# A float32 decoder layer on one core: low parts of split operands emitted a step after their conversions

## The chip, the core and the metric

The kernel runs on one core of a Trainium2 chip. The metric is device time in microseconds, the median of three runs. Engines are named as in the profile: PE (TensorE matmul), PEld (its weight loads), DVE (VectorE), ACT (ScalarE), POOL (GpSimd), SP (SyncE, here only a queue that issues DMAs).

## What is computed

One layer of a decoder over 512 tokens of 2048 features: a gated mix of sparse attention and latent attention, cross attention over 256 memory tokens, and an MLP of 8192 features. Cut to its frame:

```python
xn = rmsnorm(h, g_mix[l])
(q_a, k_c, v_c, k_s, v_s, k_w, v_w, g_nsa, c_q, c_kv, k_r,
 gate_a, gate_b) = jnp.split(xn @ w_in[l], bounds, axis=-1)
...
o_a = nsa_attention(q_a, kc, vc, ks, vs, kw, vw, gates, ...)   # 16 heads: compressed, selected, window branch
o_b = mla_attention(c_q, c_kv, k_rope, ...)                    # 16 heads from latents of 512 and 256
mixed = sigmoid(gate_a) * (o_a @ w_o_nsa[l]) + sigmoid(gate_b) * (o_b @ w_o_mla[l])
h = h + mixed @ w_out[l]
h = h + memory_cross_attention(rmsnorm(h, g_xattn[l]), rmsnorm(mem, g_mem[l]), ...)
hn = rmsnorm(h, g_mlp[l])
h = h + jnp.square(jax.nn.relu(hn @ w_ff1[l])) @ w_ff2[l]
return rmsnorm(h, g_final)
```

## The kernel before

**Split operands.** Every large product is float32 made of three products of a rounded type (fp32r): an operand x is kept as a high part, hi = round(x), and a low part, lo = round(x - hi), and `mm` (L460 to L462) adds hi·hi, hi·lo and lo·hi. `split` (L467 to L471) makes the two: a conversion on ACT writes hi, a subtraction on DVE reads x and hi and writes lo. The subtraction is emitted right after the conversion, so DVE, which works in order, stands at it until ACT has come to the conversion.

**Order.** The program is one list of instructions written out by hand; each engine takes its own in that order and waits by semaphores for the others'. A main stream of projections runs through `chunk` and `ft`; after each group of three products they call `Side.run`, which takes steps of side work at a set rate: attention steps, and "post" steps that turn a finished projection into heads.

**Weights.** `Stream` loads units of 512 KB into a ring of two raw areas (`RAW`) and splits them, half a unit per call, into a ring of three split areas (`HLB`), about two units ahead of their use: `get` splits one half, `mid`, called in the middle of a unit, the other. `done` says that a raw area is free, once both halves of its unit have been split; the load of the unit two later is issued from there, on SP's queue (in the output projection also on POOL's, adding in place). A unit is 24 full products of 512 columns in most stages.

**Heads.** `proj_post` (sparse attention), `heads_T` (latent attention) and `proj_m`'s `post` (latents) transpose 128 x 128 blocks with PE into one PSUM bank of the pool `st`, and `split` that bank. `st` has three banks in rotation; `new_st` takes the next, and the first product into it waits until its last reader is done. `proj_m` also squares the latents' rows on ACT (L1135, L1137), the four row blocks in one step.

**Attention.** `scores` makes a branch's score rows from the last block to the first, one bank each; `soft` takes a row's maximum on DVE (L609) and the exponential on ACT (L610); one step later the row is scaled on DVE (L628). In the compressed branch the compressed scores share a bank with the row's, but for the last block (512 columns, a full bank), where they take one more. `values` transposes the softmax weights in groups (`tr`, L705) into a bank, splits them, and multiplies them with the values two steps later (`pv`, L724, L726). `attend` merges the score steps of a branch with the value steps of the one before.

**The end.** The MLP is a Strassen-like scheme of products p; `prep` loads and splits weights three steps ahead (L1635, L1640), `use2` adds or subtracts a product's sums from the result rows on DVE (L1867, L1869). Around the last two products the result is normalized: `square` (ACT, L1969), `rstd`, then one half of a row block is scaled by `factor` (DVE, the gain) and `scaled` (ACT, the row's factor), the other half by `both` (DVE, L1991), each followed by the store. Rows 0 and 1 finish beside the last product but one, rows 2 and 3 in `end`.

Of the kernel before, what the change touches and what calls it, by code (L numbers as in the profile page):

```python
# [16 lines left out]
EPS = 1e-6  # L17
# [236 lines left out]
class Stream:  # L254
# [4 lines left out]
    def __init__(self, k, dram_w, order, info):  # L259
        self.k, self.dram, self.order, self.info = k, dram_w, order, info  # L260
        self.raw = [k.slots.get() for _ in range(self.RAW)]
        self.hl = [(k.slots.get(), k.slots.get()) for _ in range(self.HLB)]
        self.n = self.nd = self.ns = self.nr = self.warm = 0
# [27 lines left out]
    def done(self, t):  # L291
        return self.ns >= 2 * self.user.get(id(t), -1) + 2
# [17 lines left out]
    def _split(self, upto):  # L310
# [3 lines left out]
        while self.ns < upto and self.ns < 2 * self.last:  # L314
# [6 lines left out]
            self.k.split(HL(h[:, s], l[:, s]), self.at[n][:, s])  # L321
            self.ns += 1
            if half:
                t = self.at.pop(n)
# [14 lines left out]
    def end(self):  # L339
        for t in [*self.raw, *(t for h in self.hl for t in h)]:  # L340
            self.k.slots.put(t)

    def get(self, tag):
# [6 lines left out]
        self._split(2 * (n + self.HLB) - 1)  # L350
        c = self.info[dram(tag)][1]
# [16 lines left out]
class Side:  # L368


    def __init__(self):
# [26 lines left out]
    def run(self, n, post):  # L398
        if post and self.post is not None:
# [10 lines left out]
    def drain(self):  # L410
        self.end_post()
        while self.step():
            pass
        self.acc = 0


class Layer:
    def __init__(self, tc, ctx, a, order, info):
# [36 lines left out]
        self.side = Side()  # L455
# [19 lines left out]

    def new_st(self):
        return self.psst.tile([128, 512], F32, name="st")
# [74 lines left out]
    def heads_T(self, n, take):  # L552

        for v in range(n):
# [8 lines left out]
            self.split(h, ps[:96, :])  # L563
            take(h)
            yield

# [48 lines left out]
    def scores(self, item):  # L615
# [27 lines left out]
        def step(i):  # L643
# [5 lines left out]
            elif i >= 0 and not (i == 0 and "stats" in item):  # L649
                o, n = at(i)  # L650
                ps = self.new_st()
                pc = None
# [4 lines left out]
                elif i < 3:  # L657
                    self.mm(ps[:, :32 + n], qi, k[:, :32 + n], True, True)
                    pc, ps = ps[:, :32], ps[:, 32:32 + n]
# [6 lines left out]
                if cgate:  # L666
                    self.soft(pc, item["Pc"][:, i], self.cst[:, C_CM + i * 32:C_CM + i * 32 + 32], SC_ATT,
                              cmx[:, i:i + 1], csm[:, i:i + 1])
# [16 lines left out]
    def values(self, item):  # L685
# [6 lines left out]
        def tr(group):  # L692
# [17 lines left out]
            else:  # L710
                self.split(h[:, :o], ps[:, :o])
# [26 lines left out]
    def attend(self, items, start=None):  # L738
# [3 lines left out]
        for it in items:  # L742
# [4 lines left out]
            for f in merge(a, b, LEAD):  # L747
                f()
                yield
# [5 lines left out]
    def flush(self):  # L755
        for f in self.values(self.prev):
            f()
# [124 lines left out]
    def proj_post(self, c):  # L882
# [34 lines left out]
        for nm, x in (("q", None), ("ks", 1), ("kw", 2)):  # L917
            for i, o in at.get(nm, ()):
# [11 lines left out]
                self.split(h, ps[:96, :])  # L930
                yield
        if c == 1:
# [186 lines left out]
    def proj_m(self, rate):  # L1119
# [10 lines left out]
        def post(c):  # L1130
# [9 lines left out]
            yield  # L1140
            for j in range(3):
# [9 lines left out]
                self.split(h, ps, self.gains[:, G_Q + f:G_Q + f + 1])  # L1151
                (self.cq if f < 4 else self.ckv).append(h)
                yield
            if c:
# [416 lines left out]
class Mlp:  # L1571
# [164 lines left out]
    def run(self, out):  # L1736
# [11 lines left out]
        for p in range(last):  # L1748
# [14 lines left out]
            for j in range(4):  # L1763
# [33 lines left out]
        self.end(last, X)  # L1797
# [128 lines left out]
    def end(self, p, X):  # L1926

        k, nc = self.k, self.nc
        v = nc.vector
        for t in (2, 3):  # L1930
            self.square(t, 2)
            self.square(t, 3)
            self.factor(t, 1)
# [4 lines left out]
        self.square(2, 1)  # L1938
        for j in range(4):
# [3 lines left out]
        self.scaled(2, 1, r2)  # L1943
        self.both(2, 0, r2)
# [38 lines left out]
    def scaled(self, t, b, r):  # L1983
# [3 lines left out]
        nc.scalar.dma_start(self.out[t][:, 1024 * b:1024 * b + 1024], x)  # L1987
# [68 lines left out]
```

## Time and profile before

| | |
|---|---|
| median of 3 runs | 2831.62 us (2830.07 to 2833.07) |
| profiled execution | 2828.84 us, its span 2827.0 us, TensorE clock 0.999 |
| DMA | 460.19 MB, mean 163 GB/s |
| PE, chain that ended last | 93% of the span |

A row of the stage table gives the stage, its length, each engine's busy time with its count of instructions, the granted clock, the DMA share and the rate. Rows of waits give the sum in us, how often, and the longest. Rows of groups give busy time, mean ns of one, and the idle time of the engine before them with what ended it. Rows in order of time give start, duration, and in brackets the idle time of the engine just before. In names, `st`, `mm` and `o` are PSUM banks, `s` and `d` areas of SBUF, `PP` the softmax rows, `mx` the row maxima.

### The profile page before, as it was taken

To read this page: it belongs to the slowest core of one execution; us is meant where nothing else is said; L and a number is where in the kernel's file an instruction comes from. 1 tells how busy PE (TensorE), PEld (TensorE's weight loads), DVE (VectorE), ACT (ScalarE), POOL (GpSimd) and SP (SyncE) were. 2 spreads that over 40 slices of the span, in tenths; PEclk is the share of its full clock that TensorE was granted. 3 is DMA by queue.
4 is the path that set the end of the run, shared out by engine and by line. 5 is a ranking of instruction groups with operands and counts; after the bars stand their busy time and mean duration, and the time that the engine had idled before them with its cause. 6 is when DMAs were issued, how large, how long until landed. Compare 5 with 4: busy or idle time off the path is not lost.

```text
span 2827.0 us, 38143 instructions
## 1 busy us (share of the span) xinstructions
PE 2799.2 (99%) x14091; PEld 2378.8 (84%) x14091; DVE 1915.9 (68%) x3160; ACT 1514.7 (54%) x2611; POOL 412.8 (15%) x626
## 2 busy tenths in 40 slices
PE   9999999999999999999999999999999999999998
PEld 8888889888888888889998888888888888888886
DVE  6446666665555565556785877777766788888787
ACT  5445555544444444334566766666666644444445
POOL 4130011002010001001130111111111111111110
PEclk9999999999999999999999999999999999999999
DMA  5331112222333335559644888798888999889996
GB/s 179 96 96 61 59 54 64 60 94 91 96 101 101 97 121 192 183 182 255 161 105 142 216 221 209 204 223 212 213 211 205 229 229 226 227 225 236 239 236 164
DMA packets 151883, 460.19 MB, mean 163 GB/s; under 512 B 16144, under 2 KB 32912, under 8 KB 151696
## 3 DMA queue, kind: packets, MB, share of 16 engines
q1 hardware_dynamic: 82736, 271.05, 28.6%
q0 software_dynamic: 41472, 151.01, 28.4%
q10 hardware_dynamic: 27488, 35.70, 3.6%
q8 instruction: 110, 1.80, 0.3%
q14 instruction: 77, 0.63, 0.1%
HBM read 419.94 MB, written 37.75 MB: 162 GB/s over the span
## 4 chain that ended last, share of the span: by engine, by line
PE 93%; DVE 3%; ACT 3%; issue 1%; DMA 0%; SPq 0%; ACTq 0%; DVEq 0%
PE mm L460 12%; PE mm L462 12%; PE mm L461 12%; PE mm L1821 8%; PE mm L1823 8%; PE mm L1822 8%; PE st L1823 5%; PE st L1821 5%; PE st L1822 5%; PE st L705 2%; DVE s L468 1%; PE o L724 1%; PE mm L1422 1%; PE mm L1421 1%; PE mm L1420 1%; PE o L726 1%
## 5 line engine op out<-in xcount | busy, mean ns | idle before, releaser
L460 PE MATMUL mm<-s,s 128*128 128x512 f32 (+5 forms) x1528 | 601.2, 393 | 1.1 <-ACT s L1127 0.7
L461 PE MATMUL mm<-s,s 128*128 128x512 f32 (+5 forms) x1528 | 582.5, 381 | 0.6 <-DVE s L468 0.4
L462 PE MATMUL mm<-s,s 128*128 128x512 f32 (+5 forms) x1528 | 582.7, 381 | 0.0
L468 DVE TENSOR_TENSOR s<-s,s 128x512 fp32r<-128x512 f32 (+4 forms) x558 | 384.2, 711 | 225.5 <-ACT s L467 224.5
L467 ACT CAST s<-s 128x512 fp32r<-128x512 f32 (+4 forms) x558 | 330.0, 608 | 257.9 <-PE mm L461 84.2
L1821 PE MATMUL mm<-s,s 128*128 128x512 f32 x1024 | 400.1, 391 | 3.0 <-DVE s L1869 3.0
L1823 PE MATMUL mm<-s,s 128*128 128x512 f32 x1024 | 398.5, 389 | 0.0
L1822 PE MATMUL mm<-s,s 128*128 128x512 f32 x1024 | 398.5, 389 | 0.0
L1640 DVE TENSOR_TENSOR s<-s,s 128x1024 fp32r<-128x1024 f32 x234 | 284.1, 1222 | 151.7 <-ACT s L1635 151.2
L462 PEld LDWEIGHTS mm<-s,s 128*128 128x128 f32 x1528 | 287.2, 188 | 53.4 <-DVE s L471 0.4
L461 PEld LDWEIGHTS mm<-s,s 128*128 128x128 f32 x1528 | 288.6, 189 | 40.5 <-DVE s L468 2.1
L460 PEld LDWEIGHTS mm<-s,s 128*128 128x128 f32 x1528 | 287.8, 188 | 40.8 <-ACT s L870 1.3
L1635 ACT CAST s<-s 128x1024 fp32r<-128x1024 f32 x234 | 241.9, 1048 | 128.5 <-DMA s<-wts 111.5
L610 ACT ACTIVATE PP<-PP,mx 128x512 f32<-128x512 f32 (+2 forms) x208 | 116.3, 559 | 285.2 <-DVE mx L609 285.2
L1821 PE MATMUL st<-s,s 128*128 128x512 f32 x672 | 263.1, 391 | 0.0
L1823 PE MATMUL st<-s,s 128*128 128x512 f32 x672 | 261.7, 389 | 0.0
L1822 PE MATMUL st<-s,s 128*128 128x512 f32 x672 | 261.4, 389 | 0.0
L1821 PEld LDWEIGHTS mm<-s,s 128*128 128x128 f32 x1024 | 192.3, 188 | 42.6 <-issue 3.4
L1635 ACT CAST s<-d 128x1024 fp32r<-128x1024 f32 x138 | 143.2, 1048 | 155.9 <-DMA d<-wts 141.6
L1823 PEld LDWEIGHTS mm<-s,s 128*128 128x128 f32 x1024 | 192.3, 188 | 40.0
L1822 PEld LDWEIGHTS mm<-s,s 128*128 128x128 f32 x1024 | 192.3, 188 | 39.2
L468 DVE TENSOR_TENSOR s<-st,s 128x384 fp32r<-128x384 f32 (+2 forms) x201 | 123.7, 621 | 123.8 <-ACT s L467 123.1
(342 smaller groups left out, 4813.9 us busy)
## 6 DMA issues: line engine op xcount, KB each, us to landing
s<-wts SPq DMA_DIRECT2D x312, 512.0 KB, 3.8
s<-wts POOLq DMA_DIRECT2D x149, 512.0 KB, 8.3
d<-wts POOLq DMA_DIRECT2D x91, 512.0 KB, 8.6
PP<-wts POOLq DMA_DIRECT2D x48, 512.0 KB, 8.6
d<-wts SPq DMA_DIRECT2D x47, 512.0 KB, 7.8
d_u<-s ACTq DMA_DIRECT2D x64, 256.0 KB, 5.2
PP<-wts SPq DMA_DIRECT2D x28, 512.0 KB, 8.1
d<-d_u SPq DMA_DIRECT2D x19, 512.0 KB, 8.8
```

Source lines behind the costliest of these rows:

```text
L460: t.matmul(ps, a.hr, b.hr, start=first, stop=False)
L461: t.matmul(ps, a.hr, b.lr, start=False, stop=False)
L462: t.matmul(ps, a.lr, b.hr, start=False, stop=last)
L467: nc.scalar.copy(o.hr, src)
L468: nc.vector.tensor_sub(o.lr, src, o.hi)
L610: nc.scalar.activation(p, p, AF.Exp, bias=mx, scale=-1.0, accum_out=sm)
L705: nc.tensor.transpose(ps[:rows, o:o + 128], p, self.ident)
L1635: self.nc.scalar.copy(t.hr, self.raw[i])
L1640: self.nc.vector.tensor_sub(t.lr, r, t.hi)
L1821: m(ps, a.hr, b.hr, start=first, stop=False, skip_group_check=True)
L1822: m(ps, a.hr, b.lr, start=False, stop=False, skip_group_check=True)
L1823: m(ps, a.lr, b.hr, start=False, stop=last, skip_group_check=True)
```

## The change

- `Stream._split` emits the conversion alone and remembers the half; the new `_low` emits the subtraction of the half before (all of them for a unit that `get` hands out). `done` now counts subtractions (`nl`), and the load of a later unit and the release of an area move into `_low`.
- `split_late` does the same for heads, latents and softmax weights: it emits the conversion and puts the subtraction on a list with the count of `st` banks taken so far and a number of groups, `runs`. `tick`, called by every `Side.run`, emits those whose groups have passed (2 for heads and latents); `attend` and `flush` emit before each attention step all whose number is used up (softmax weights, 0); `new_st` emits whatever still reads the bank that it is about to give out; `settle` at the end of a post step emits the rest.
- In the compressed branch the last block's compressed scores go into columns 416 to 448 of the third block's bank, one step later, and take no bank of their own.
- `proj_m`'s squares: one row block per step, four steps for one.
- At the end: the last weights' low part (`prep`), the first two rows' `both` and the gain products (`factor`) move behind the subtractions of the product before (`use2`) and behind the third row's additions; the third row's `both` moves behind the last addition; its other half is stored by SP's queue instead of ACT's.

```diff
     def done(self, t):
-        return self.ns >= 2 * self.user.get(id(t), -1) + 2
+        return self.nl >= 2 * self.user.get(id(t), -1) + 2
...
-            self.k.split(HL(h[:, s], l[:, s]), self.at[n][:, s])
+            o = HL(h[:, s], l[:, s])
+            self.k.nc.scalar.copy(o.hr, self.at[n][:, s])
+            self.late.append((n, half, o, s))
             self.ns += 1
+            self._low(1)
             if half:
-                t = self.at.pop(n)
+                self._dma(n + self.LOOK)
+
+    def _low(self, keep):
+
+        while len(self.late) > keep:
+            n, half, o, s = self.late.popleft()
+            t = self.at[n]
+            self.k.nc.vector.tensor_sub(o.lr, t[:, s], o.hi)
+            self.nl += 1
+            if half:
+                tag = self.order[n]
+                del self.at[n]
                 if tag[0] == "wo" and tag[1] in (4, 5, 6) and not any(t is r for r in self.raw):
...
         self._split(2 * (n + self.HLB) - 1)
+        while self.nl < 2 * n + 2:
+            self._low(len(self.late) - 1)
...
+    def split_late(self, o, src, scale=None, runs=0):
+        nc = self.nc
+        if scale is None:
+            nc.scalar.copy(o.hr, src)
+            low = lambda: nc.vector.tensor_sub(o.lr, src, o.hi)
+        else:
+            nc.scalar.activation(o.hr, src, AF.Copy, scale=scale)
+            low = lambda: nc.vector.scalar_tensor_tensor(o.lr, src, scale, o.hi, op0=OP.mult, op1=OP.subtract)
+        self.lows.append([self.n_st, runs, low])
+
+    def settle(self, which=lambda e: True):
+        now, self.lows = [e for e in self.lows if which(e)], [e for e in self.lows if not which(e)]
+        for _, _, low in now:
+            low()
+
+    def tick(self):
+        for e in self.lows:
+            e[1] -= 1
+        self.settle(lambda e: e[1] == 0)
+
     def new_st(self):
+        self.n_st += 1
+        self.settle(lambda e: e[0] <= self.n_st - 3)
         return self.psst.tile([128, 512], F32, name="st")
...
-            self.split(h, ps[:96, :])
+            self.split_late(h, ps[:96, :], runs=2)
...
+                    pcs = [(i, ps[:, :32])]
+                    if i == 2:
+                        pcs.append((3, ps[:, 416:448]))
+                        self.mm(ps[:, 416:448], q[:, 384:512], k[:, :32], True, True)
...
-                    pc = self.new_st()[:, :32]
-                    self.mm(pc, qi, k[:, :32], True, True)
...
-                self.split(h[:, :o], ps[:, :o])
+                self.split_late(h[:, :o], ps[:, :o])
...
             for f in merge(a, b, LEAD):
+                self.settle(lambda e: e[1] <= 0)
                 f()
                 yield
...
                     nc.gpsimd.tensor_copy(r[:, 416:448], r[:, 384:416])
-            yield
+                yield
...
-                self.split(h, ps, self.gains[:, G_Q + f:G_Q + f + 1])
+                self.split_late(h, ps, self.gains[:, G_Q + f:G_Q + f + 1], runs=2)
...
-                    self.scaled(j - 2, 1, r[:, j - 2:j - 1])
-                    self.both(j - 2, 0, r[:, j - 2:j - 1])
+                    self.scaled(j - 2, 1, r[:, j - 2:j - 1], self.nc.scalar)
...
-            if p == last - 1:
-                self.prep(4 * last + 3)
             (self.use2 if layer else self.use1)(p, ps)
...
-    def end(self, p, X):
+    def end(self, p, X, r):
...
+        self.prep(4 * p + 3)
+        for t in range(2):
+            self.both(t, 0, r[:, t:t + 1])
         for t in (2, 3):
             self.square(t, 2)
             self.square(t, 3)
-            self.factor(t, 1)
         for j in range(4):
             self.part(p, j, X, [0])
         self.use2(p, X, [0])
         self.square(2, 0)
         self.square(2, 1)
+        self.factor(2, 1)
+        self.factor(3, 1)
...
-        self.scaled(2, 1, r2)
-        self.both(2, 0, r2)
+        self.scaled(2, 1, r2, nc.sync)
...
         v.tensor_add(c, self.cols[:, 14:15], self.cols[:, 15:16])
+        v.tensor_add(c, self.cols[:, 12:13], c)
+        v.tensor_scalar(c, c, 1.0 / D, EPS, op0=OP.mult, op1=OP.add)
         v.tensor_add(self.row(3, 1), X[3], self.row(3, 1))
         self.square(3, 1)
-        v.tensor_add(c, self.cols[:, 12:13], c)
-        v.tensor_scalar(c, c, 1.0 / D, EPS, op0=OP.mult, op1=OP.add)
+        self.both(2, 0, r2)
```

More of the change, by code (lines that the diff above doesn't have):

```diff
@@ L262, in __init__ @@
         self.hl = [(k.slots.get(), k.slots.get()) for _ in range(self.HLB)]
-        self.n = self.nd = self.ns = self.nr = self.warm = 0
+        self.n = self.nd = self.ns = self.nl = self.nr = self.warm = 0
+        self.late = deque()
         self.log = []
@@ L339, in end @@
     def end(self):
+        self._low(0)
         for t in [*self.raw, *(t for h in self.hl for t in h)]:
@@ L368, with __init__ @@
 class Side:
-    def __init__(self):
+    def __init__(self, k):
+        self.k = k
         self.q = deque()
@@ L398, in run @@
     def run(self, n, post):
+        self.k.tick()
         if post and self.post is not None:
@@ L413, in drain @@
             pass
+        self.k.settle()
         self.acc = 0
@@ L454, in __init__ @@
         self.prev = None
-        self.side = Side()
+        self.side = Side(self)
+        self.lows, self.n_st = [], 0
     def mm(self, ps, a, b, first, last):
@@ L562, in heads_T @@
             h = self.slot_hl(96)
-            self.split(h, ps[:96, :])
+            self.split_late(h, ps[:96, :], runs=2)
             take(h)
             yield
+        self.settle()
     def chunk(self, name, c, ncols, evac, rate, nk=16, per=2, xs=None, on_k=None):
@@ L651, in step @@
                 ps = self.new_st()
-                pc = None
+                pcs = []
                 qi = q[:, i * 128:i * 128 + 128]
@@ L658, in step @@
                     self.mm(ps[:, :32 + n], qi, k[:, :32 + n], True, True)
-                    pc, ps = ps[:, :32], ps[:, 32:32 + n]
+                    pcs = [(i, ps[:, :32])]
+                    if i == 2:
+                        pcs.append((3, ps[:, 416:448]))
+                        self.mm(ps[:, 416:448], q[:, 384:512], k[:, :32], True, True)
+                    ps = ps[:, 32:32 + n]
                 else:
                     self.mm(ps, qi, k[:, 32:], True, True)
-                    pc = self.new_st()[:, :32]
-                    self.mm(pc, qi, k[:, :32], True, True)
                 mask = self.cst[:, C_MASK:C_MASK + 256] if mem else self.cst[:, C_MASK + 512 - n:C_MASK + 512]
                 self.soft(ps, P[:, o:o + n], mask, SC_XA if mem else SC_ATT, mx[:, i:i + 1], sm[:, i:i + 1])
-                if cgate:
-                    self.soft(pc, item["Pc"][:, i], self.cst[:, C_CM + i * 32:C_CM + i * 32 + 32], SC_ATT,
-                              cmx[:, i:i + 1], csm[:, i:i + 1])
+                for j, pc in pcs:
+                    self.soft(pc, item["Pc"][:, j], self.cst[:, C_CM + j * 32:C_CM + j * 32 + 32], SC_ATT,
+                              cmx[:, j:j + 1], csm[:, j:j + 1])
             if i < 3:
@@ L756, in flush @@
         for f in self.values(self.prev):
+            self.settle(lambda e: e[1] <= 0)
             f()
@@ L929, in proj_post @@
                     h = h[:, 32:] if nm == "ks" else h
-                self.split(h, ps[:96, :])
+                self.split_late(h, ps[:96, :], runs=2)
                 yield
+        self.settle()
         if c == 1:
@@ L1796, in run @@
                     self.nc.sync.dma_start(self.gain[b], self.gain_rows(b))
-        self.end(last, X)
+        self.end(last, X, r)
     def part(self, p, j, ps, ts):
@@ L1981, in factor, with scaled @@
         self.nc.vector.tensor_mul(self.R[t, b], self.R[t, b], self.gain[b])
-    def scaled(self, t, b, r):
+    def scaled(self, t, b, r, queue):
         x, nc = self.R[t, b], self.nc
         nc.scalar.activation(x, x, AF.Copy, scale=r)
-        nc.scalar.dma_start(self.out[t][:, 1024 * b:1024 * b + 1024], x)
+        queue.dma_start(self.out[t][:, 1024 * b:1024 * b + 1024], x)
     def both(self, t, b, r):
```

1 line of the change is left out of this document (added).

## The prediction, made before the changed kernel was run

> **What bounds the kernel now.** I read the page's busy table first, then busy time by stage, then who PE waited for in the one stage where it idles, then the order of time around such waits.
>
> ```profile
> PE 2799.2 (99%) x14091; PEld 2378.8 (84%) x14091; DVE 1915.9 (68%) x3160; ACT 1514.7 (54%) x2611; POOL 412.8 (15%) x626
> ```
> ```profile
> 0.00:110.00 110.00, 108.19 (x498) 91.45 (x499) 62.31 (x84) 58.98 (x105) 36.16 (x61) 1.00 0.49 155
> ...
> 200.00:565.00 365.00, 353.36 (x1964) 306.50 (x1963) 247.75 (x815) 204.82 (x597) 42.23 (x132) 1.00 0.19 60
> 565.00:1075.00 510.00, 509.52 (x2580) 432.38 (x2579) 285.63 (x694) 242.48 (x543) 32.40 (x80) 1.00 0.32 103
> ...
> 2210.00:2780.00 570.00, 570.00 (x2520) 472.19 (x2520) 470.18 (x493) 272.59 (x284) 106.11 (x122) 1.00 0.93 232
> 2780.00:2827.00 47.00, 34.77 (x153) 28.18 (x151) 36.68 (x58) 24.41 (x49) 1.75 (x2) 0.95 0.44 129
> ```
>
> The first two numbers of a stage row are its length and PE's busy time. TensorE sets the time: nothing here removes a product of weight, so only its holes can be won. They are in two places: 365.00 - 353.36 = 11.64 us in the stage 200 to 565 (sparse attention beside projection), and 12.23 us at the end. MLA (0.48 us of hole) and the MLP (none) have nothing to give. So the edits of the heads' low parts in MLA and of the weights after it can gain nothing; they can only cost. PE's waits inside 200 to 565:
>
> ```profile
> PE st L1144 <- DVE s L468: 3.6, 3, 2.0
> PE st L460 <- DVE s L468: 3.5, 7, 0.7
> PE st L705 <- DVE s L468: 2.1, 5, 0.5
> ...
> PE st L1144 <- DVE d L471: 0.4, 1, 0.4
> ```
>
> Columns: sum, times, longest. These 16 waits make 9.6 of the 11.64 us, all at the first product into an "st" bank (three banks), all for a low part on DVE. The rest is for ACT's evacuations and is left alone. A recorded wait is too short, because ends are modelled: in the tail's rows below, products of 0.39 us start 0.23 us apart, so the idle time begins 0.16 us late. The 16 waits cost about 9.6 + 16 x 0.16 = 12.2 us. One of them in order of time, DVE, ACT and PE put together:
>
> ```profile
> 263.09 0.69 DVE L468 TENSOR_TENSOR s<-s,s 128x512 fp32r<-128x512 f32 x1 [1.05 <-ACT s L467]
> 263.81 0.69 DVE L609 CUSTOM_DVE_ANT_0 PP<-st,cst 128x512 f32<-128x512 f32 x1
> ```
> ```profile
> 264.55 0.72 ACT L610 ACTIVATE PP<-PP,mx 128x512 f32<-128x512 f32 x1 [1.49 <-DVE mx L609]
> ...
> 265.27 0.46 ACT L467 CAST s<-st 128x384 fp32r<-128x384 f32 x1
> ```
> ```profile
> 265.76 0.56 DVE L468 TENSOR_TENSOR s<-st,s 128x384 fp32r<-128x384 f32 x1 [1.25 <-ACT s L467]
> ```
> ```profile
> 266.37 0.38 PE L460 MATMUL st<-d,s 96*128 96x256 f32 x1 [0.60 <-DVE s L468]
> ```
>
> At 263.09 DVE does a weight's low part; it has stood idle 1.05 us for that weight's conversion, with the row maximum of a score (L609) queued behind. The exponential waits for the maximum, the conversion of the transposed softmax weights stands behind the exponential on ACT, their low part behind that, and PE for the bank. One idle wait travels through four instructions and comes out as 0.60 us on PE.
>
> **The change part by part.**
>
> Low parts on DVE in 200 to 565, grouped (count, busy, mean ns, idle before):
>
> ```profile
> L468 DVE TENSOR_TENSOR s<-s,s 128x512 fp32r<-128x512 f32 (+3 forms) x83 | 53.6, 646 | 38.1 <-ACT s L467 37.8
> ```
> ```profile
> L468 DVE TENSOR_TENSOR s<-st,s 128x384 fp32r<-128x384 f32 x52 | 28.8, 554 | 28.8 <-ACT s L467 28.8
> ...
> L468 DVE TENSOR_TENSOR s<-st,s 128x512 fp32r<-128x512 f32 x26 | 17.9, 689 | 11.1 <-ACT s L467 11.1
> ```
>
> *Weights, heads, softmax weights.* No instruction is added: 83 weight halves, 26 full-width transposes and 52 softmax blocks keep their conversion and subtraction. A weight's subtraction comes one call later, its conversion long done, so the 37.8 us for which DVE stood in front of those 83 (0.46 us each) goes. A head's comes two groups of three products later; most of its 11.1 us goes. A softmax block's is emitted just ahead of the next attention step, still in front of that step's maximum, so in the chain above it keeps its place and its 28.8 us mostly stays. What is late next is that loop itself (maximum, exponential, conversion, subtraction: 0.69 + 0.72 + 0.46 + 0.56 us and the read-out between). In the chain above 1.05 us of idle goes and 0.60 us on PE needed it. Bounds for the 12 waits at L460 and L705 (5.6 + 12 x 0.16 = 7.5 us): 0 and 7.5. I take two thirds, **-5.0**, since the removed idle per weight (0.46) is about the mean wait (5.6 / 12 = 0.47), and the heads' idle comes on top.
>
> *Squares.* Four squares of the latent stood in one step:
>
> ```profile
> 493.21 0.52 ACT L1135 ACTIVATE s<-s 128x384 f32<-128x384 f32 x1
> 493.64 0.19 ACT L1135 ACTIVATION_READ_ACCUMULATOR s<-s 128x1 f32 x1
> ```
> ```profile
> 495.19 0.59 DVE L468 TENSOR_TENSOR s<-s,s 128x416 fp32r<-128x416 f32 x1 [2.85 <-ACT s L467]
> ```
> ```profile
> 496.31 0.66 PE L1144 MATMUL st<-cst,s 128*128 128x128 f32 x4 [2.02 <-DVE s L468]
> ```
>
> Each holds ACT about 0.65 us, the four 2.6 us, with DVE idle 2.85 and PE 2.02 behind them. One per step leaves 0.65 us at a time, which other steps cover. Of the four L1144 waits (3.6 + 0.4 + 4 x 0.16 = 4.6 us) I take **-3.5**, bounds -4.6 and 0; the remaining 1.1 us are banks.
>
> *Banks.* The last row's compressed scores move into the bank of the third row's (three narrow products earlier, one bank fewer per head): a gain I put inside the two thirds. Against it, a head's bank is held two groups longer. Trace of before has no such wait; bounds 0 and, for 26 transposes, one maximum and one subtraction each (0.69 + 0.69) = 36 us. I take **+1.2**, near zero: a head's two branches have 22 steps of which 14 take a bank, about one step to a group, so the third bank after a transpose is asked for some 4.7 groups later. The Trainium skill ("Perfetto Trace Analysis", section Optimization Strategy) says that bubbles which repeat can mean that there is too little SBUF or PSUM to allocate the next tile. All 16 waits are of that kind here, which speaks against holding banks longer; by that rule the time is the last rival's.
>
> *Start.* A raw area frees only after its subtraction, so a weight's load on SP leaves a call later. In the first chunk ACT already waits for loads:
>
> ```profile
> L467 ACT CAST s<-s 128x512 fp32r<-128x512 f32 (+1 forms) x23 | 13.5, 603 | 12.2 <-DMA s<-wts 9.4 <-PE mm L462 2.8
> ```
> ```profile
> 27.40 1.78 DVE L471 SCALAR_TENSOR_TENSOR s<-s,gains,s 128x512 fp32r<-128x512 f32 x1
> ```
>
> Between a second half's conversion and its subtraction now stands one subtraction of x (L471, up to 1.78 us), so a load leaves up to two us later, ACT waits as much longer, and x's next part, queued behind it, is late. PE's holes in 0 to 110 are 1.81 us now, so there is cover, but not for half a unit (12 x 0.23 = 2.7 us). Bounds 0 and +2.7; I take **+0.8**. The same delay in the memory's keys and values, where each load follows the subtraction of the unit two before, costs nothing as long as no DVE work stands between; I put it at 0, bounds -0.5 and +1. The Trainium skill ("SBUF — State Buffer", section SBUF: two separate sides) explains the 1.78: VectorE with two SBUF inputs and GpSimd exclude each other; the trace has POOL additions at that time and agrees, and by the rule what matters for the start is which subtractions meet them, not how many are moved.
>
> *Tail.* The last product cannot start until the former's sums have left their banks:
>
> ```profile
> 2803.03 0.39 PE L1822 MATMUL mm<-s,s 128*128 128x512 f32 x1
> 2803.26 0.39 PE L1823 MATMUL mm<-s,s 128*128 128x512 f32 x1
> 2806.66 0.47 PE L1821 MATMUL mm<-s,s 128*128 128x512 f32 x1 [3.02 <-DVE s L1869]
> ```
> ```profile
> 2803.50 1.28 DVE L1991 SCALAR_TENSOR_TENSOR s<-s,rx,s 128x1024 f32<-128x1024 f32 x1
> 2804.69 1.22 DVE L1640 TENSOR_TENSOR s<-PP,s 128x1024 fp32r<-128x1024 f32 x1
> 2805.83 2.48 DVE L1869 TENSOR_TENSOR s<-s,mm 128x512 f32<-128x512 f32 x4
> ...
> 2816.49 1.28 DVE L1991 SCALAR_TENSOR_TENSOR s<-s,rx,s 128x1024 f32<-128x1024 f32 x1
> ...
> 2819.31 0.21 DVE L503 TENSOR_SCALAR rs<-PP 128x1 f32<-128x1 f32 x1 [0.54 <-ACT s L1969]
> ```
>
> PE ends at 2803.65. The two final scalings (L1991, the row shows the second) and a low part (L1640) now come after the four subtractions, so L1869 starts at about 2803.8 instead of 2805.83 and PE resumes 0.83 us after that start, as before: 2804.6, **2.05 us earlier**. Not all reaches the end. The moved low part and scalings fill DVE to 2809.9, the two gain products follow the first additions to 2813.5, and the third row's factor comes at about 2815.2. Its scaling holds ACT to 2816.4, the last sum's square follows to 2817.2, while DVE does the third row's scaling (1.28 us, now after the last addition) to 2817.7; L503 then, against 2819.31: **-1.6**, bounds -2.1 and 0. The output moved from ACT's queue to SP's passes only other outputs there.
>
> Sum: -5.0 - 3.5 + 1.2 + 0.8 - 1.6 = -8.1 us against the profiled execution (2827.0 us of span, 2828.84 in all), which lies 2.8 us under the median of the timed runs. On the median, 2831.62: **2823.5 us**.
>
> **The rivals.** Below 0.2% (5.7 us) a measurement of this kernel can't tell a change from none.
> - All waits go (-12.2 and -2.0, banks and start free): 2817.4. For it: the chain shown loses more idle time than PE waited. Against: the softmax blocks' 28.8 us stay. Chance 0.15.
> - It does not do what it says: the softmax blocks keep their place and the loop through them, not the weights' idle, made the waits. Then -2 of the 7.5, -2.5 of the squares, +1.2, +0.8, -1.0: -3.5, 2828.1. For it: 1.25 us of the example's idle is the loop's. Chance 0.26.
> - Banks: a head's late low part becomes the wait. It decides where the third bank after a transpose is asked for within two groups. If so for half of the 26, at 1.38 us: +17.9, with the forecast's other terms (-9.3) +8.6: 2840.2. For it: every wait of the stage is for an st bank. Against: 0.64 banks per step. Chance 0.07.
>
> **How the numbers follow.** The forecast has 0.52, with a range of its own of 2820 to 2828. Faster by over 0.2% means below 2825.9: the first rival and most of the forecast (0.15 + 0.47) and little of the second (0.02), 0.64; slower by over 0.2% is the last, 0.07; the rest 0.29. The range leaves out the deepest part of the first rival and the last: 2817 to 2831.
>
> **What would show it.** Right: PE's holes in 200 to 565 fall from 11.64 to about 5 us; L468 on s<-s there waits under 5 us for ACT instead of 37.8; no L1144 wait over 1 us; the last product starts about 1 us after the former's end. Wrong: new st waits at L924 or L560 or after them (banks), holes between 10 and 40 us (start), or the softmax blocks' 28.8 us unchanged with PE's waits still there.

## The result, and the profile after

The changed kernel takes 2816.76 us (median of 4 runs, 2816.15 to 2816.86), the kernel before 2830.85 (4 runs, 2828.94 to 2833.07): a ratio of 0.995, interval 0.9932 to 0.9967. The medians lie 14.1 us apart, the profiled executions 12.1 (2828.84 and 2816.75 us; spans 2827.0 and 2815.0). The prediction said 2823.5 us, from 2817 to 2831: the sign was right, the forecast gain too small, and the time lies 0.24 us under the range.

Lines have moved: L460 to L462 are now L482 to L484, the transposes L705 and L1144 are L752 and L1194, a weight's conversion and subtraction are L323 and L335, a late low part's L501 and L502 (with a gain L504 and L505), an immediate one's L489 and L490, the last product's subtractions L1917.

The stages of the changed kernel (stage, length, busy time of PE first, granted clock third from the end):

```profile
0.00:110.00 110.00, 107.41 (x496) 90.74 (x497) 63.29 (x83) 58.51 (x105) 33.28 (x61) 1.00 0.47 153
200.00:565.00 365.00, 360.11 (x2017) 317.93 (x2016) 253.52 (x841) 213.62 (x614) 41.74 (x132) 1.00 0.20 62
...
2210.00:2780.00 570.00, 569.47 (x2513) 471.43 (x2512) 474.74 (x498) 270.29 (x283) 105.25 (x121) 1.00 0.92 231
```

The hole in 200 to 565 is 365.00 - 360.11 = 4.89 us, where it was 11.64; 3.6 of it are one new wait. Who PE waited for there (sum, times, longest):

```profile
PE st L482 <- DVE s L502: 3.6, 1, 3.6
PE st L752 <- DVE s L502: 1.0, 3, 0.6
PE mm L482 <- ACT s L919: 0.2, 1, 0.2
```

Sixteen waits for an `st` bank have become four, but one of them is 3.6 us long, and it is new. DVE's groups in the stage (count, busy, mean ns, idle before), two of the kernel before, then those of the changed kernel:

```profile
L468 DVE TENSOR_TENSOR s<-st,s 128x384 fp32r<-128x384 f32 (+2 forms) x89 | 54.0, 610 | 47.7 <-ACT s L467 47.7
L609 DVE CUSTOM_DVE_ANT_0 PP<-st,cst 128x512 f32<-128x512 f32 (+3 forms) x109 | 52.6, 482 | 20.5 <-PE st L462 19.9
```
```profile
L502 DVE TENSOR_TENSOR s<-st,s 128x384 fp32r<-128x384 f32 (+2 forms) x92 | 56.1, 611 | 49.8 <-ACT s L501 49.1
L335 DVE TENSOR_TENSOR s<-s,s 128x512 fp32r<-128x512 f32 (+3 forms) x86 | 55.6, 648 | 1.6 <-ACT s L323 1.3
L654 DVE CUSTOM_DVE_ANT_0 PP<-st,cst 128x512 f32<-128x512 f32 (+3 forms) x112 | 54.3, 485 | 32.6 <-PE st L484 32.1
```

The weights' idle is gone (1.3 us for 37.8). The first group taken apart by shape, the heads' row (96 rows of 512) of the kernel before first, then the changed kernel:

```profile
L468 DVE TENSOR_TENSOR s<-st,s 96x512 fp32r<-96x512 f32 x11 | 7.5, 686 | 7.8 <-ACT s L467 7.8
```
```profile
L502 DVE TENSOR_TENSOR s<-st,s 128x384 fp32r<-128x384 f32 x54 | 30.1, 557 | 35.1 <-ACT s L501 34.7
L502 DVE TENSOR_TENSOR s<-st,s 128x512 fp32r<-128x512 f32 x27 | 18.7, 692 | 14.5 <-ACT s L501 14.4
L502 DVE TENSOR_TENSOR s<-st,s 96x512 fp32r<-96x512 f32 x11 | 7.5, 680 | 0.1
```

The heads' idle is gone too. The 49.1 us that are left stand in front of softmax weights alone: the groups of `values` are 384, 384 and 512 columns wide. There DVE idles more than before, yet PE hardly waits: most of that idle time is now DVE waiting for work, not work waiting for DVE. The row maximum (L654) points the same way: its idle grew from 19.9 to 32.1 us and is ended by PE.

Where the time went is best read from one and the same product of the main stream in both traces. The table is worked out so: start in the changed kernel minus start in the kernel before, in us; "again" is a second run of the changed kernel.

| start in the kernel before | 41 | 149 | 367 | 524 | 571 | 575 | 1084 | 1235 | 2661 | 2728 | 2817 | end |
|---|---|---|---|---|---|---|---|---|---|---|---|---|
| changed | +0.36 | +0.15 | -6.01 | -12.43 | -16.05 | -10.57 | -11.02 | -9.87 | -9.93 | -9.10 | -12.37 | -12.06 |
| again | +0.21 | +0.01 | -6.09 | -12.53 | -16.16 | -9.95 | -10.04 | -9.00 | -9.04 | -9.04 | -12.30 | -11.99 |

By 571 us 16.4 us are won after the start (from +0.36 to -16.05); 5.5 are lost at once; 1.15 go in the memory's keys and values; 0.83 in the MLP, which did not come again; 3.3 are won at the last product. Up to 571 us these two executions of one program differ by 0.15 us at most, later by up to 1.

The loss between 571 and 575 is this (changed kernel, in order of time, ACT, DVE and PE):

```profile
552.22 1.28 ACT L548 ACT_TABLE_LOAD   x1
...
556.32 1.28 ACT L1218 ACT_TABLE_LOAD   x1 [1.48 <-DVE s L1217]
557.61 0.63 ACT L1218 ACTIVATE s<-s 128x512 f32<-128x512 f32 x1
...
558.64 0.62 ACT L323 CAST s<-s 128x512 fp32r<-128x512 f32 x1 [0.40 <-ACT s L1218]
559.16 0.47 ACT L501 CAST s<-st 128x384 fp32r<-128x384 f32 x1
```
```profile
555.55 0.69 DVE L1217 TENSOR_TENSOR s<-mm,rbc 128x512 f32<-128x512 f32 x1
...
559.67 0.56 DVE L502 TENSOR_TENSOR s<-st,s 128x384 fp32r<-128x384 f32 x1 [2.83 <-ACT s L501]
```
```profile
555.49 0.49 PE L752 MATMUL st<-cst,PP 128*128 128x128 f32 x3
...
560.28 0.39 PE L482 MATMUL st<-d,s 96*128 96x256 f32 x1 [3.61 <-DVE s L502]
```

The post steps of the second chunk of latents were five and are eight: four squares, three transposes, the root. A gate calls eight post steps, one on every second of its 16 groups, so the root (L548 with its table load, and DVE's Newton steps to 555.55) now stands right before the gate's own evacuation (L1217, then the tanh with another table load). The softmax weights transposed at 555.49 are converted only at 559.16, behind all that, and PE stands for their bank. Behind the wait stands half a clock:

```profile
556.90:560.30 3.40, 0.02 (x1) 0.02 (x1) 0.63 (x2) 2.33 (x4) 0.00 (x0) 1.00 0.64 202
...
561.60:564.60 3.00, 3.00 (x12) 2.52 (x12) 2.41 (x7) 1.74 (x5) 0.00 (x0) 0.53 0.00 0
564.60:567.00 2.40, 2.40 (x15) 2.01 (x14) 0.69 (x1) 1.00 (x3) 0.00 (x0) 1.00 0.56 142
```

PE counts as busy there, at a clock of 0.53. The wait and the clock make 5.5 us together (3.6 recorded, 0.16 for the modelled end of the product before it, and 1.7, the half of 3.41 us at half clock).

And the tail, DVE's rows in order of time:

```profile
2791.93 1.22 DVE L1691 TENSOR_TENSOR s<-s,s 128x1024 fp32r<-128x1024 f32 x1
2793.07 2.48 DVE L1917 TENSOR_TENSOR s<-s,mm 128x512 f32<-128x512 f32 x4
2795.46 1.22 DVE L1691 TENSOR_TENSOR s<-PP,s 128x1024 fp32r<-128x1024 f32 x1
...
2807.26 0.21 DVE L547 TENSOR_SCALAR rs<-PP 128x1 f32<-128x1 f32 x1
```

PE does not wait at the last product at all; it starts products 0.23 us apart throughout.

### The profile page after: what moved, and what is told of

Read it like the earlier page. It is cut to its first block, busy times and chain, and to the rows that moved or that the text cites. A ratio compares the mean times of both kernels' runs of the same rounds, so it can differ in the third digit from the quotient of the medians.

```text
span 2815.0 us, 38108 instructions
## 1 busy us (share of the span) xinstructions
PE 2796.0 (99%) x14091; PEld 2381.6 (85%) x14091; DVE 1907.7 (68%) x3160; ACT 1515.3 (54%) x2611; POOL 405.0 (14%) x626
## 4 chain that ended last, share of the span: by engine, by line
PE 92%; DMA 2%; DVE 2%; issue 2%; ACT 1%; POOL 0%; SPq 0%; ACTq 0%; POOLq 0%; DVEq 0%
PE mm L482 12%; PE mm L484 12%; PE mm L483 12%; PE mm L1871 8%; PE mm L1870 8%; PE mm L1869 8%; PE st L1871 5%; PE st L1869 5%; PE st L1870 5%; PE st L752 2%; DMA s<-wts 1%; PE o L771 1%; PE st L483 1%; PE st L484 1%; PE mm L1473 1%
## 5 line engine op out<-in xcount | busy, mean ns | idle before, releaser
L482 PE MATMUL mm<-s,s 128*128 128x512 f32 (+5 forms) x1528 | 602.2, 394 | 0.4 <-ACT s L323 0.3
L484 PE MATMUL mm<-s,s 128*128 128x512 f32 (+5 forms) x1528 | 583.9, 382 | 0.3 <-DVE s L493 0.3
L323 ACT CAST s<-s 128x512 fp32r<-128x512 f32 (+4 forms) x536 | 315.9, 606 | 276.2 <-DMA s<-wts 145.5
L335 DVE TENSOR_TENSOR s<-s,s 128x512 fp32r<-128x512 f32 (+4 forms) x536 | 367.7, 704 | 85.1 <-ACT s L323 83.2
L484 PEld LDWEIGHTS mm<-s,s 128*128 128x128 f32 x1528 | 287.5, 188 | 53.8 <-DVE s L493 0.9
L482 PEld LDWEIGHTS mm<-s,s 128*128 128x128 f32 x1528 | 288.2, 189 | 40.5 <-ACT s L919 0.9
L1691 DVE TENSOR_TENSOR s<-d,s 128x1024 fp32r<-128x1024 f32 x138 | 167.7, 1220 | 49.9 <-ACT s L1686 49.9
```

The lines of the kernel that those rows point to most:

```text
L323: self.k.nc.scalar.copy(o.hr, self.at[n][:, s])
L335: self.k.nc.vector.tensor_sub(o.lr, t[:, s], o.hi)
L482: t.matmul(ps, a.hr, b.hr, start=first, stop=False)
L484: t.matmul(ps, a.lr, b.hr, start=False, stop=last)
L1691: self.nc.vector.tensor_sub(t.lr, r, t.hi)
```

## Experiments

Each kernel is the changed one with an edit, unless it says otherwise; spans are those of one profiled execution, and most of these kernels were executed only once, with the kernel before at 2831.7 to 2832.4 us on the same chips. Differences under about 1 us are therefore not told apart. "Later at 511" means the start of the product that the changed kernel starts at 511.7 us, the one of 524 us above.

**One part alone.** Kernel before, plus only the weights' late low parts (`_split` and `_low` as in the change), or only the heads' and latents':

```diff
-                self.split(h, ps[:96, :])
+                self.split_late(h, ps[:96, :], runs=2)
...
-                self.split(h, ps, self.gains[:, G_Q + f:G_Q + f + 1])
+                self.split_late(h, ps, self.gains[:, G_Q + f:G_Q + f + 1], runs=2)
```

> Kernel before plus one part of the change: the weights' low parts a call later; all else as before. Profiled executions: before 2828.84 us, after 2816.75. Theory A (the weights' subtractions, at which DVE stood idle 37.8 us in 200 to 565, carried most of PE's waits for low parts at the transposes and products): -4 to -6 us against before, PE's hole in 200 to 565 falls from 11.64 to 6 to 7.5 us; of it +0.4 us are lost at the start and about +1.1 in the memory's keys and values. Rival B (the heads' low parts carried them): -1 to -2 us, the hole stays above 9 us.

> Kernel before plus one part of the change: the heads' and latents' low parts two groups later; all else as before. Theory A (the weights carried the waits): -0.5 to -2 us, hole in 200 to 565 at 9.5 to 11 us. Rival B (the heads carried them): -4 to -5 us, hole at 6 to 7.5 us. Banks held two groups longer: no new wait of over 0.5 us at a first product into a bank in either theory.

The weights alone: span 2821.8 us, 5.2 less; 4.8 ahead at 524, 7.2 at 575, and 1.4 lost again by 1235: theory A. They are worth more than that up to 524, since this execution has a half clock behind a pause of 1.89 us, which the kernel before has not, and which costs about 1.7 us (half of 3.41):

```profile
492.80:496.20 3.40, 3.40 (x15) 3.24 (x14) 2.62 (x9) 2.30 (x10) 0.00 (x0) 0.50 0.00 0
```

The heads alone: span 2832.5 us, **5.5 more**. Neither theory had a loss. Of it 0.7 stands already at 41 us, where nothing of the heads runs, and 3.1 come between 524 and 571 us, with the 2.4 us wait below and a half clock behind it. The first waits of the heads alone, in 200 to 572:

```profile
PE st L752 <- DVE s L490: 4.4, 7, 0.9
PE st L1194 <- DVE s L490: 3.3, 2, 2.0
PE st L752 <- DVE d L505: 2.4, 1, 2.4
```

The third row is the prediction's banks rival: a latent's late low part still reads the bank that PE wants. Its conversion ends at 557.73, but DVE comes to the subtraction only at 559.93, behind a weight's, for whose conversion it waits until 559.32. The first row is more of the old kind of wait than before (2.1 us at L705); that it too comes from late subtractions landing behind immediate ones was not followed wait by wait.

**One part taken out.** The weights:

```diff
             self.ns += 1
-            self._low(1)
+            self._low(0)
```

> The changed kernel with the weights' low parts again right behind their conversions. Alone, the weights' part moved the first product after 520 us 4.8 us forward against the kernel before; the heads' part alone moved it 1.8 us back. Theory A (the weights' subtractions in front of DVE are what makes the other late subtractions wait, so the parts do not add up): at 511 us (changed kernel) it is 6 to 9 us later than the changed kernel, the start and the stretch of the memory's keys and values are faster by 0.3 to 0.5 and by 0.7 to 1.4 us, the whole is 4 to 8 us longer. Rival (the parts add up): 4 to 5 us later at 511 us and 3 to 4 us longer in all.

Span 2843.3 us: 28.3 more than the changed kernel, 16 more than the kernel before. 22.9 us later at 511, over four times what the weights bring alone: the parts do not add up, as theory A has it, but by far more than its 9. (One half clock more than in the changed kernel, at 241 us, is about 1.7 of it.) Waits in 200 to 572, and one of them (DVE and ACT):

```profile
PE st L752 <- DVE s L502: 10.7, 11, 1.9
PE st L482 <- DVE s L502: 3.1, 6, 0.7
```
```profile
239.65 0.66 DVE L335 TENSOR_TENSOR s<-s,s 128x480 fp32r<-128x480 f32 x1 [2.22 <-ACT s L323]
240.22 0.55 DVE L502 TENSOR_TENSOR s<-st,s 128x384 fp32r<-128x384 f32 x1
```
```profile
238.19 0.94 ACT L501 CAST s<-st 96x512 fp32r<-96x512 f32 x2
239.02 0.59 ACT L323 CAST s<-s 128x480 fp32r<-128x480 f32 x1
```

The softmax weights' conversion (second of the two L501) ends at 239.13, and DVE is idle. But their subtraction was put off and stands behind a weight's, whose conversion comes after it on ACT: it runs at 240.22, and PE waits 1.89 us. An immediate subtraction in front of late ones hands its wait to them.

The softmax weights, the heads and latents (the edit above turned round), and the shared bank of the compressed scores, each taken out:

```diff
-                self.split_late(h[:, :o], ps[:, :o])
+                self.split(h[:, :o], ps[:, :o])
```
```diff
-                    if i == 2:
-                        pcs.append((3, ps[:, 416:448]))
-                        self.mm(ps[:, 416:448], q[:, 384:512], k[:, :32], True, True)
...
                     self.mm(ps, qi, k[:, 32:], True, True)
+                    pc = self.new_st()[:, :32]
+                    self.mm(pc, qi, k[:, :32], True, True)
+                    pcs = [(i, pc)]
```

> The changed kernel with the softmax weights' low parts again right behind their conversions. By 511 us the changed kernel is 4.7 us further ahead than the weights' part and the spread squares explain. Theory A (the softmax weights: other low parts and maxima pass while ACT converts): 3 to 4.5 us later than the changed kernel at 511 us, waits of 0.3 to 0.7 us at L482 and L752 are back. Rival B (the prediction's: they keep their place in the loop, so the 4.7 us are the heads' or the banks'): less than 1 us later.

> The changed kernel with the heads' and latents' low parts again right behind their conversions. Of the 12.4 us that the changed kernel is ahead at 511 us (524 in the kernel before) the runs gave the weights 4.8 (alone), the softmax weights 4.5, the squares 2.9, the banks 1.0 (each taken out): 13.2 without the heads. Theory A (nothing is left for the heads once the weights wait no more): -0.5 to +1 us against the changed kernel at 511 us and in all, beside what the memory's keys and values vary (1 us). Rival (DVE's 11.1 us of idle in front of the heads' low parts cost PE something, as the prediction has it): +1.5 to +4 us.

> The changed kernel with a bank of its own again for the last block's compressed scores. Theory A (one bank fewer per head is worth little, since 14 banks of a head's 22 steps remain): 0 to 1 us later than the changed kernel at 511 us. Rival C (it carries the 4.7 us that the weights and squares leave): 3 to 4.5 us later.

| taken out | later at 41 us | later at 511 us | span |
|---|---|---|---|
| softmax weights | +0.10 | +4.52 | 2818.0 |
| heads, latents | +0.15 | +3.21 | 2818.5 |
| shared bank | +0.90 | +1.05 | 2815.3 |

With the weights late, the softmax weights are worth 4.4 us (theory A) and the heads 3.1, less what stands at 41 us; theory A fell for the heads, the rival held. The bank is worth 0.15, which is not told from nothing: the rest of its 1.05 stands already at 41 us, where nothing of it runs. Rival C fell. In the run without late softmax weights, waits at L752 are back:

```profile
PE st L752 <- DVE s L490: 3.1, 6, 0.8
```

**The squares, and the long wait.** The squares in one step again, and, as a test of the cause, the root two post steps later:

```diff
                     nc.gpsimd.tensor_copy(r[:, 416:448], r[:, 384:416])
-                yield
+            yield
```
```diff
             self.settle()
             if c:
+                yield
+                yield
                 nc.vector.tensor_add(self.ssq[:, :4], self.ssq[:, :4], self.ssq[:, 4:])
```

> The changed kernel with one part undone: the squares of all four row blocks in one step again. Theory A (the changed kernel's one long wait, 3.6 us at 560.28 at a transpose of softmax weights, comes from the squares spread over four steps, which push the root and its table load beside the gate's tanh): that wait and the half clock after it are gone, one wait of 2 to 3 us at the latents' transposes is back per chunk of latents; total within 1 us of the changed kernel. Rival (the wait comes from late low parts and held banks): a wait of over 2 us stays near 560 and the total is 3 to 4 us over the changed kernel.

> The changed kernel with the latents' root (table load, square roots, Newton steps) two post steps later, past the first gate's evacuation. Theory A (the wait of 3.6 us at 560.28 is the root standing right before the gate's tanh): the wait falls under 1.5 us, no half clock follows, the first product after 564 us is 3 to 4.7 us earlier than in the changed kernel, the whole 2 to 5 us shorter. Rival (the spread squares and held banks make it): a wait of over 2.5 us within 5 us of the same place, no gain.

Without the spread the long wait is gone, and waits of 1.9 and 1.5 us are back, one beside each chunk of latents: 3.3 us later at 511, 6.85 just before the place of the long wait, 1.4 behind it, span 2815.7: theory A, but for the length of the waits. Not all of the 6.85 is the spread's: 0.39 stands at 41 us, and behind the second wait this run has a half clock that the kernel before has not there:

```profile
546.60:550.00 3.40, 3.32 (x12) 3.06 (x13) 2.29 (x10) 0.59 (x1) 0.00 (x0) 0.51 0.02 5
```

It costs about 1.7 us (half of 3.41). So the spread wins about 4.8 us against the kernel before, an estimate, and gives 5.5 back. With the root later all of PE's waits in 200 to 572 are

```profile
PE st L752 <- DVE s L502: 1.4, 4, 0.6
PE mm L482 <- ACT s L919: 0.2, 1, 0.2
```

and behind the place of the long wait it is 5.4 us ahead of the changed kernel, more than theory A's 3 to 4.7; the span is 2810.9 us, 4.1 less: theory A.

**The tail as before**, the core of it:

```diff
                     self.scaled(j - 2, 1, r[:, j - 2:j - 1], self.nc.scalar)
+                    self.both(j - 2, 0, r[:, j - 2:j - 1])
...
+            if p == last - 1:
+                self.prep(4 * last + 3)
             (self.use2 if layer else self.use1)(p, ps)
...
-        self.prep(4 * p + 3)
-        for t in range(2):
-            self.both(t, 0, r[:, t:t + 1])
```

> The changed kernel with one part undone: the order of the end as before (last low part, first two rows' scalings and gain products ahead of the subtractions, third row's scaling ahead of the last addition). Theory A (the banks of the product before come free in turn, so that with the subtractions first the last product need not wait at all): +2.8 to +3.3 us against the changed kernel, a wait of about 3.0 us is back at the last product's first matmul. The prediction's sum: +1.6 us.

PE's last product waits again, and that costs 3.3 us; another 1.6 come from half a clock behind the wait, which the kernel before did not have. The windows behind the wait, of this run and of the kernel before:

```profile
2801.70:2805.50 3.80, 3.80 (x11) 2.98 (x10) 2.42 (x3) 0.99 (x4) 0.00 (x0) 0.56 0.07 28
```
```profile
2808.10:2812.00 3.90, 3.90 (x19) 3.23 (x18) 2.77 (x4) 1.04 (x4) 0.00 (x0) 1.00 0.08 30
```

Theory A, by the wait's own 3.3. Span 2822.3 us, 7.3 more: 4.9 here, about 1.0 at the long wait, where the half clock lasts 6.83 us and not 3.41 (the second run of the changed kernel has the same, and loses 0.94 by it), 1.3 in the memory's keys and values, the rest in the MLP. Those vary between executions.

**Where late weights cost.** Low parts of weights immediate in the first two chunks and from the mix on, with the root later; then the same, but late again in cross attention:

```diff
-            self._low(1)
+            self._low(self.keep)
...
             if c == 1:
+                self.W.keep = 1
...
+    L.W.keep = 0
     L.mix()
     L.w_out()
+    L.W.keep = 1
     L.cross(1.4).run(a["out"])
```

`keep` begins at 0; the first version lacks the last line added here.

> The changed kernel with the root two post steps later and the weights' low parts right behind their conversions where no side work runs: the first two chunks, and from the mix on (memory's keys and values, cross attention). Theory A (a load that leaves half a unit later is what the start and the memory's keys and values lose): against the run with the root alone 0.1 to 0.5 us less at 40 us, and the loss of 0.5 to 1.4 us between 1150 and 1235 us gone; 2809 to 2810.5 us of span less 0.5 to 1.5, so 2809 to 2810.5 us in all (profiled) and no wait for a weight's low part there. Rival (the memory's stretch is bound by the loads whatever their start): as the run with the root alone, 2810.9 us of span.

> The changed kernel with the root two post steps later and the weights' low parts right behind their conversions in the first two chunks and from the mix to the last output of the memory's keys and values, but late again in cross attention. Theory A (an immediate low part of a weight in front of late ones of softmax weights cost the run with the same rule in cross attention too 1.0 us of PE's wait at 1505.81): that wait is gone, span 2809 to 2810 us, timed 5.5 to 7.5 us below the changed kernel and 19.5 to 22 us below the one before. Rival: the loss sits elsewhere and the span stays at 2810.7 us or above.

> The changed kernel once more, unaltered, for its time beside the run above and for how much the profile differs between two executions of one program. Theory A: the wait of 3.6 us near 560 with the half clock behind it and the tail come again within 0.2 us, the memory's keys and values, the start and the MLP's waits for weights differ by up to 1 us each, since they hang on when loads land; 2816 to 2818 us. Rival: the differences between the runs at 511 us that the study leans on (1 to 23 us) are of the size by which two executions differ, then over 1 us there.

ACT's conversions of weights in 1150 to 1235 us and what ended their idle time, in the kernel before, the changed one, and the last version:

```profile
L467 ACT CAST s<-s 128x512 fp32r<-128x512 f32 x49 | 28.6, 619 | 48.8 <-DMA s<-wts 24.9 <-PE mm L461 16.8 <-DMA s<-d_mla 3.5
```
```profile
L323 ACT CAST s<-s 128x512 fp32r<-128x512 f32 x46 | 26.4, 619 | 53.6 <-DMA s<-wts 44.1 <-PE mm L483 5.4 <-PE mm L484 2.1
```
```profile
L323 ACT CAST s<-s 128x512 fp32r<-128x512 f32 x46 | 27.1, 620 | 52.2 <-PE mm L483 25.4 <-DMA s<-wts 22.3 <-PE mm L484 2.8
```

With late low parts ACT waits for loads 44.1 us instead of 24.9. Against PE's products, the changed kernel's loads leave 3.8 to 5.2 us later between 1104 and 1158 us (worked out load by load); in the heads alone, where the weights are immediate, 0.0. PE's loss between 1084 and 1235 us goes with it: in the nine traces with late weights there PE loses 0.2 to 2.5 us against the kernel before, in the four others with immediate ones 0.0. The first `keep` version wins the 1.15 us there, and loses 2.3 after it up to 2661 us. Of them 1.07 are one wait at 1505.81 in cross attention, where an immediate weight stands before late softmax weights, and 0.9 come in the MLP, which varies:

```profile
1504.46 0.69 DVE L335 TENSOR_TENSOR s<-s,s 128x512 fp32r<-128x512 f32 x1 [0.89 <-ACT s L323]
1505.07 1.28 DVE L502 TENSOR_TENSOR s<-st,s 128x512 fp32r<-128x512 f32 x2
```

Its span is 2810.7 us. The second has neither loss (theory A; it lies under the span it named, since the start came 0.8 us earlier as well): span 2807.5 us, a median of 2809.45 us in 5 runs (2809.29 to 2811.08), against 2816.28 for the changed kernel (5 runs, 2815.96 to 2816.82) and 2830.58 for the kernel before (9 runs, 2829.09 to 2832.62) on the same chip. The ratios to the kernel before are 0.9926 (0.9914 to 0.9939) and 0.9949 (0.9935 to 0.9962). It beats both. The second run of the changed kernel agrees with theory A: the long wait of 3.6 us and the tail came again, and at 511 us it lies 0.10 from the first.

## Why the prediction was right, and where it was wrong

A gain was forecast for the right reason, DVE standing in front of weights' low parts. The step that failed is the first term of the sum, -5.0 + 1.2 us: it took two thirds of 7.5 us and put the softmax weights' late low parts at nothing, and the runs show about -11.6 us, to which the softmax weights, with the weights late, bring 4.4. Two losses that the sum does not have, 5.5 us behind the spread squares and 1.15 in the memory's keys and values, hid a part of this.

| step | forecast | profiled |
|---|---|---|
| weights, heads, softmax weights, banks | -5.0 + 1.2 | about -11.6 |
| squares | -3.5 | about +0.7 (-4.8 and +5.5) |
| start | +0.8 | +0.4 |
| MLA | 0 | -0.5 |
| memory's keys and values | 0 | +1.15 |
| MLP | 0 | +0.8 |
| tail | -1.6 | -3.0 |
| sum | -8.1 | -12.1 |

The first row is the 16.4 us up to 571 less the 4.8 that are estimated for the squares, the others come from the table of products.

**Weights, heads, softmax weights: the chain right, the size wrong, and outside the bounds.** Three errors. The size of the holes was read from recorded waits: 9.6 us, with 0.16 added to each for the modelled ends, 12.2. Taken from one start to the next, PE's products in that stretch of the kernel before lose 16.75 us over their usual distance, in 32 gaps of over 0.11 us each. Two waits for ACT's evacuations (0.7 and 0.4), which the prediction leaves alone, have become one of 0.2, and the slower starts of 0.1 to 0.2 us behind many waits mostly went too. Then, "28.8 us mostly stays" was true of DVE's idle time and wrong of PE: the softmax weights are worth 4.4 us. The idle time in front of an instruction says what the engine waited for, not what was lost by it. And the rows were misread: the 26 of 128x512 with 11.1 us are softmax weights too, not heads. The heads are 96x512, with 7.8 us before and 0.1 after; that their sum is near 11.1 (another six have 3.2) is chance. The two thirds came from two like means (0.46 and 0.47 us) and had nothing else behind them.

**Squares: the gain near its bound, and the next thing late was not looked for.** The four waits were priced at 4.6 us at most, and the spread wins about 4.8. That four steps more move the root to the gate's evacuation, which costs 5.5, could have been counted from the code: five steps, eight slots, eight steps.

**Banks:** right for the changed kernel, which has no such wait; that the term is near zero holds only because the weights are late. The Trainium skill ("Perfetto Trace Analysis", Optimization Strategy) says that bubbles which repeat can mean too few buffers; here they went with the same three banks, because the late thing was the subtraction that frees them.

**Start:** that loads leave later is shown, by 1.8 to 3.7 us against PE's products between 13 and 43 us, where the prediction had up to two. What it costs is not. At 41 us the nine traces with late weights lie 0.2 to 1.3 us behind the kernel before, and the four others with immediate weights at -1.0, -0.2, +0.6 and +0.7. Whether the POOL additions beside these subtractions matter was not tried.

**Memory's keys and values:** "costs nothing as long as no DVE work stands between" is wrong. The subtraction is emitted only at the next call, and the load leaves with it, here 3.8 to 5.2 us later, whatever DVE does.

**Tail: mis-sized.** The forecast let the four subtractions start when the whole former product had ended. Its four banks are finished in turn, 0.68 us apart, so the subtractions run from 2793.07, while that product still runs until 2794.54, and PE's 3.0 us go altogether. At the end of the span 3.0 of the 3.3 arrive.

**From span to median.** The 2.8 us between the profiled execution and the median of the kernel before were carried over whole. The changed kernel has no such distance (2816.75 and 2816.76): its runs spread 0.7 us, those of the kernel before 4.1. Of the 6.7 us between the forecast 2823.5 and 2816.76, 4.0 lie in the profiled execution and 2.8 here. Why the kernel before spreads more was not tried. The half clock is a candidate, no more: of the four traces with its 3.0 us pause at the last product one has it.

**The signs named for it.** The hole fell to 4.89 us, the weights' idle to 1.3, no wait at L1194 is over 1 us: as forecast. That the hole meets "about 5" is luck: all but about 1.3 us of the old one went, and 3.6 are a wait that nobody forecast. The last product starts with no wait at all, and the softmax blocks' idle stayed without PE's waits.

**The rivals.** All waits go (2817.4, chance 0.15): nearly what happened, with other terms: more won, 5.5 lost again. That its number fits to 0.6 us is luck. The second, that the softmax loop made the waits and the change would not touch it, fell: with the loop's idle time still there the waits went, though 4.4 us hung on the softmax weights' low parts. The banks rival has its mechanism shown in the heads alone (2.4 us at one latent) and does not decide here; its 26 transposes are the misread rows, there are 17 heads and 6 latents in the stage.

## What to carry to other kernels

Where an in-order engine takes subtractions behind another engine's conversions, put off all that meet in one stretch or none: one that stays immediate makes those put off behind it wait for its conversion (the weights left immediate: 28 us here). Put them off only where other work stands between, since what a late subtraction frees, a bank or an area to load into, comes free later too. And when one step is cut into several, count where its last piece lands.

## What the runs showed of the hardware

The granted TensorE clock of these 14 traces is either whole or half. While products run it is halved twelve times, at most twice in a trace: ten times for 3.41 us, and twice for 6.83 us (near 559 us in the second run of the changed kernel and in the tail as before, where PE still stood idle for over 1 us in the first 3.41). Two rows, of the weights taken out and of the heads alone:

```profile
241.40:244.80 3.40, 3.40 (x13) 2.81 (x13) 2.55 (x7) 1.56 (x5) 0.00 (x0) 0.50 0.00 0
```
```profile
561.70:565.00 3.30, 3.30 (x12) 2.61 (x12) 2.25 (x9) 0.38 (x1) 0.00 (x0) 0.54 0.30 117
```

The starts of these halvings lie on a grid. Counted in steps of 3.413 us from the half clock that ends each trace, all twelve starts are whole numbers to 0.001 (659.0 in the changed kernel, 761.0 and 660.0 with the weights taken out). Cut into the steps of this grid, PE's idle time by its records separates the cases: the half clock begins at the end of a step with 1.89 us of idle time or more, twelve of twelve, and never at the end of one with 1.81 us or less. So a pause counts by how it falls on the grid. The 3.02 us pause before the last product of the kernel before is cut into 1.81 and 1.21 us and cost no clock; the 3.01 us pause of the tail as before has 1.97 us in one step and cost it. A pause of 1.89 us that falls into one step was enough, and one of 2.02 us, cut into 0.34 and 1.68, was not.

The Trainium skill ("TensorE: Matmul & The Clock Gate", What's actually happening) has the clock halved after at least one idle window of about 3.4 us that runs free, and restored after a busy one. The free-running window and its length agree with these traces (3.413 us). That the window has to be idle throughout does not: 1.89 us of it were enough. A pause of 2 us can so cost another 1.7 us, and what it costs differs between executions of one program: behind the same pause of 3.61 us the two runs of the changed kernel have 3.41 and 6.83 us of half clock.
